# Two buffers for the first snapshot of a pair, and one address phase for both sides of SBUF

## The chip, the cores and the metric

The kernel runs on one core of one Trainium2 chip. The metric is the device time of one execution in microseconds (us), lower is better. Three executions of the kernel before took 2232.48, 2235.39 and 2237.11 us; their median is 2235.39. A fourth one was recorded by the profiler, and every row below is of that one.

The engines: PE is the matrix engine, which multiplies a moving tile (in SBUF) with weights loaded into it (also from SBUF) and sums into PSUM; PEld is its weight load. DVE, ACT and POOL are the vector, scalar and general engines; SP issues most of the DMAs.

## The reference

A decoder trunk of two layers on x of 1024 tokens by 1024 features, float32. Layer 0 mixes tokens with a chunked causal gate, layer 1 with causal differential attention over shared keys and values. Behind each mixer stands the same feed-forward block:

```python
def swiglu(h, w_gu, w_down):
    gu = h @ w_gu                       # 1024 x 1024 by 1024 x 5632
    g, u = jnp.split(gu, 2, axis=-1)
    return (jax.nn.silu(g) * u) @ w_down   # 1024 x 2816 by 2816 x 1024

for l in range(2):
    x = x + (gmlp_mixer if l < 1 else diff_attention)(rms_norm(x, ...), ...)
    x = x + swiglu(rms_norm(x, ffn_norm[l]), ffn_w_gu[l], ffn_w_down[l])
return rms_norm(x, final_norm)
```

## The kernel before

**Stages.** By the profiled execution's clock, in us: the gate branch z (34 to 92), its multiplier u (107 to 205), their output projection (205 to 310), feed-forward up of layer 0 (310 to 771), down of layer 0 (to 985), the v projection (997 to 1087), K and Q projections inside the attention (1112 to 1500), output (to 1560), up of layer 1 (1560 to 2009), down of layer 1 (to the end).

**Three products for one.** Each float32 operand is split into a high and a low part (tiles named ...h and ...l, or `w_hi` and `w_lo`): ACT casts the high part, DVE subtracts it. High times high, high times low and low times high are summed in PSUM. All these are matmuls of 512 or 256 columns (L39 is the one line through which all of PE's work goes).

**Up.** `w_gu` is cut into 11 chunk pairs j; each has a gate part (g, index 0) and an up part (u, index 1). A product by Strassen's method (Winograd's form) takes the place of eight block products. Pair 0 is done by `unit`, pairs 1 to 10 by `pair`. Names in `pair`: `B11`, `T1`, `T2`, `T3`, `B22` are blocks or sums of blocks of the activations, and at once the names of the products with them; two further products, with `B21` and `T4`, are cut once more (class `Finer`, products `mul` 1 to 7 of 256 columns, whose moving tiles are also called `fine`). A pair has 120 matmuls of 512 columns (12 for each of B11, T1, T2, T3, B22, for g and for u) and 84 of 256 columns. A product's weights are made just before it by `weight` (L304 to 310 of the kernel before): a copy into a stage (`row`, `near` or `po`, L306), a cast (L307), a subtraction (L308), into one of four `wg` buffers.

**Snapshots.** PSUM is short, so ACT copies a bank into SBUF by `snap` (L318 to 321) as soon as its product is done, and the next product is summed into the same bank:

```python
def snap(name, src):
    r = op.tile([P, 512], F32, name=name)
    A.copy(r, src)
    return r
```

The pool `op` has one buffer for each name, so c110 of a pair can be written only when the pair before is through with its c110. In a pair the names are c110 (after B11 of g), c220 (after T1 of g), c120 (after T2 of g: T2 is summed onto B11 in the bank of c110), c111 (after B11 of u), c221, c210, c121, c211. DVE later adds further banks to them (`add`, L461), and at the end of a pair POOL multiplies g by u (`store`, L340) and forms four sums (`store_sums`, L349), which SP writes to memory (`ascr`). These sums are written into the tiles c221, c121, c111, c211 (s1 to s4), and read c110, c120, c210, c220. In time this happens while the next pair has begun.

**What sets the order.** A scheduler that simulates the engines puts the instructions of all engines in an order at build time, from dependencies, buffers and modelled durations. PE's order is written by hand in the other stages; in pairs 1 to 10 the scheduler orders PE too. Every engine then runs its own list in order and waits where its next instruction is not yet free to go.

**Sides of SBUF.** Pools are laid from the left end of SBUF upwards or (function `right`, L78) from the right end downwards. In the kernel before, the left tiles that PE reads begin at multiples of 64 bytes, the right ones at 32 bytes past such multiples. Which tiles of activations stand right: in layer 0 T3, B22, B21, B11; in layer 1 T4, T3, B22 (L242, L244); `wg` is left in both. In z and u the token tiles are right and the weights left. In the v projection the weights are left, the first half of the tokens left and the second half right. In K and Q the weights are right, the tokens again half and half.

Of the kernel before, what the change touches and what calls it, by code (L numbers as in the profile page):

```python
# [9 lines left out]
F32 = mybir.dt.float32  # L10
# [6 lines left out]
P = 128  # L17
# [51 lines left out]
def trunk(ctx, tc, out, x, a_norm, w_z, w_u, gv, w_spT, b_sp, w_out, ffn_norm, w_gu, w_down,  # L69
# [5 lines left out]
    def pool(stack, name, bufs=1, **kw):  # L75
        return stack.enter_context(tc.tile_pool(name=name, bufs=bufs, reuse_waits="tile", **kw))

    def right(stack, name, bufs=1):  # L78
        return pool(stack, name, bufs, side="right")

    const = ctx.enter_context(tc.tile_pool(name="const", bufs=1))
    sm = pool(ctx, "small", 4)
    xs = pool(ctx, "xs", 8)

# [156 lines left out]
    def ffn_up(entry, layer, ascr):  # L241

        with ExitStack() as st:
# [5 lines left out]
            w1, op, sp, raw1, raw0 = (ps[n] for n in ("w1", "s", "S", "raw1", "raw0"))  # L249
# [49 lines left out]
            def weight(src, name):  # L299

                w = w1.tile([P, 2, *src.shape[1:]], F32R, name="wg")
                if name[1] == layer and name[2] == 0:
                    T.note(line, name, split(w[:, 0], w[:, 1], src))
                    return w  # L304
                near = stage().rearrange("p (k c) -> p k c", c=P)[:, :src.shape[1]]
                A.copy(near, src)  # L306
                A.copy(w[:, 0], src)  # L307
                T.note(line, name, V.tensor_tensor(w[:, 1], near, w[:, 0].bitcast(F32), op=ALU.subtract))  # L308
                return w

            def multiply(ps, w, b, start, name):
                for k in range(4):
                    with T.keep(line, name + (k,)):
                        T.matmul(ps, w[:, 0, k], hi[b][:, k], start=start and k == 0, stop=False, skip_group_check=not start)
                        T.matmul(ps, w[:, 0, k], lo[b][:, k], start=False, stop=False, skip_group_check=not start)
                        T.matmul(ps, w[:, 1, k], hi[b][:, k], start=False, stop=k == 3, skip_group_check=not start)

            def snap(name, src):  # L318
                r = op.tile([P, 512], F32, name=name)
                A.copy(r, src)  # L320
                return r

# [12 lines left out]
            def sum4(j, gu, a12, s2, s4):  # L335
                T.note(line, ("S4", layer, j, gu), G.tensor_tensor(s4, a12, s2, op=ALU.subtract))
# [15 lines left out]
            def unit(gu, res):  # L352

                def product(ps, src, b, start):
                    multiply(ps, weight(src, ("w", layer, 0, gu, b)), b, start, (layer, 0, gu, b))
                a11, a12, a22, s1, s2, s3, s4 = sums(0, gu)
                Z, Y, X = (p.tile([P, 512], F32, name="mm") for p in mmp)
                product(X, a11, "B11", True)
                c11 = snap(f"c11{gu}", X)
                yield  # L360
                product(Y, a12, "B21", True)
                T.note(line, ("c11", layer, 0, gu), V.tensor_tensor(c11, c11, Y, op=ALU.add))
                yield
                product(Z, s1, "T1", True)
                c22 = snap(f"c22{gu}", Z)
                sum4(0, gu, a12, s2, s4)
                yield
                product(X, s2, "T2", False)
                c12 = snap(f"c12{gu}", X)
                yield  # L370
                product(X, s3, "T3", False)
                V.tensor_tensor(c22, c22, X, op=ALU.add)
                yield
                product(Z, s4, "B22", False)
                V.tensor_tensor(c12, c12, Z, op=ALU.add)
                yield
                product(X, a22, "T4", False)
                res += [c11, c12, X, c22]
# [70 lines left out]
            def pair(j):  # L449

                c0, c1 = slice(0, 256), slice(256, 512)
                A_ = [sums(j, gu) for gu in range(2)]
                Z, X = ([mmp[i].tile([P, 512], F32, name="mm") for _ in range(n)] for i, n in ((0, 1), (2, 2)))
                W = mmp[0].tile([P, 2, 256], F32, name="mm")
                Z.append(mmp[0].tile([P, 512], F32, name="mm"))

                def product(ps, src, b, gu, start):
                    multiply(ps, weight(src, ("w", layer, j, gu, b)), b, start, (layer, j, gu, b))

                def add(c, ps):  # L460
                    V.tensor_tensor(c, c, ps, op=ALU.add)  # L461
                (a11g, a12g, a22g, s1g, s2g, s3g, s4g), (a11u, a12u, a22u, s1u, s2u, s3u, s4u) = A_
                product(X[0], a11g, "B11", 0, True)
                c11g = snap("c110", X[0])
                product(Z[0], s1g, "T1", 0, True)
                c22g = snap("c220", Z[0])
                sum4(j, 0, a12g, s2g, s4g)
                product(X[0], s2g, "T2", 0, False)
                c12g = snap("c120", X[0])
                product(X[1], a11u, "B11", 1, True)  # L470
                c11u = snap("c111", X[1])
                product(X[0], s3g, "T3", 0, False)
                add(c22g, X[0])
                product(Z[0], s4g, "B22", 0, False)
                add(c12g, Z[0])
                product(Z[1], s1u, "T1", 1, True)
                c22u = snap("c221", Z[1])
                sum4(j, 1, a12u, s2u, s4u)
                if j == 1:
                    finer("B21")  # L480
                    finer("T4")
                fa = Finer(j, "B21", a12g, a12u, (W[:, 0], W[:, 1]))
                add(c11g[:, c0], fa.mul(1))
                add(c11g[:, c0], fa.mul(2))
                fb = Finer(j, "T4", a22g, a22u, (X[0][:, c0], X[1][:, c0]))
                x = fb.mul(1)
                fb.mul(2)
                c21g = snap("c210", X[0])
                add(c21g[:, c0], x)
                product(X[1], s2u, "T2", 1, False)  # L490
                c12u = snap("c121", X[1])
                c21u = op.tile([P, 512], F32, name="c211")
                if j == 1:
                    names = [("d", layer, "T4", 3), ("f", layer, "B21")] + [(s, layer, 1, 0) for s in ("S1", "S2", "S3")]
                    T.order(line, names + [("S1", layer, 1, 1), ("S4", layer, 1, 0), ("f", layer, "T4")])
                for f, cg, cu in ((fa, c11g, c11u), (fb, c21g, c21u)):
                    f.weights(5)
                    z = f.mul(5)
                    if f is fa:
                        add(cu[:, c1], z)  # L500
                    else:
                        A.copy(cu[:, c1], z)
                for f, cg, cu in ((fa, c11g, c11u), (fb, c21g, c21u)):
                    f.weights(6)
                    add(cg[:, c1], f.mul(6))
                    add(cg[:, c1], f.mul(3))
                for c in (c11g, c21g, c22g, c12g):
                    A.activation(c, c, AF.Silu)
                product(X[1], s3u, "T3", 1, False)
                add(c22u, X[1])  # L510
                for f, cg, cu in ((fa, c11g, c11u), (fb, c21g, c21u)):
                    f.weights(7)
                    x = f.mul(7)
                    if f is fa:
                        both = cu.rearrange("p (i c) -> p i c", i=2)
                        V.tensor_tensor(both, both, x.unsqueeze(1).broadcast_to([P, 2, 256]), op=ALU.add)
                    else:
                        A.copy(cu[:, c0], x)
                        add(cu[:, c1], x)
                    x = f.mul(4)  # L520
                    if f is fa:
                        add(cu[:, c0], x)
                add(c21u, X[1])
                store(j, c11g, c11u, 0)
                store(j, c22g, c22u, 6)
                store(j, c21g, c21u, 5)
                product(Z[1], s4u, "B22", 1, False)
                add(c12u, Z[1])
                store(j, c12g, c12u)
                store_sums(j, c11g, c12g, c21g, c22g, (c22u, c12u, c11u, c21u))  # L530
# [312 lines left out]
    with ExitStack() as front:  # L843
# [190 lines left out]
        X = [mmp.tile([P, 512], F32, name="mm") for _ in range(4)]  # L1034
# [45 lines left out]
    with ExitStack() as mid:  # L1080
# [4 lines left out]
        with ExitStack() as att:  # L1085
# [34 lines left out]
            op = pool(att, "o", 2)  # L1120
# [367 lines left out]
```

## Time and profile before

| | |
|---|---|
| median of three runs | 2235.39 us |
| profiled execution | 2241.67 us |
| its span, first to last instruction | 2239.9 us |
| PE busy | 2138.2 us, 95% |
| DVE, ACT, POOL busy | 65%, 54%, 44% |
| mean granted TensorE clock | 0.988 of full speed |

The profiled execution is 6.3 us longer than the median. Times in the rows count from the first instruction of the span. A bracket at the end of a row of a timeline says how long the engine had nothing to do before that instruction and what ended it.

### The profile page before, as it was taken

To read this page: it belongs to the slowest core of one execution; us is meant where nothing else is said; L and a number is where in the kernel's file an instruction comes from. 1 tells how busy PE (TensorE), PEld (TensorE's weight loads), DVE (VectorE), ACT (ScalarE), POOL (GpSimd) and SP (SyncE) were. 2 spreads that over 40 slices of the span, in tenths; PEclk is the share of its full clock that TensorE was granted. 3 is DMA by queue.
4 is the path that set the end of the run, shared out by engine and by line. 5 is a ranking of instruction groups with operands and counts; after the bars stand their busy time and mean duration, and the time that the engine had idled before them with its cause. 6 is when DMAs were issued, how large, how long until landed. Compare 5 with 4: busy or idle time off the path is not lost.

```text
span 2239.9 us, 30192 instructions
## 1 busy us (share of the span) xinstructions
PE 2138.2 (95%) x10640; PEld 1773.1 (79%) x10640; DVE 1452.2 (65%) x2541; ACT 1218.3 (54%) x2436; POOL 976.3 (44%) x856
## 2 busy tenths in 40 slices
PE   9999888999999999999999999998899999999997
PEld 7888666888888778878788888887588888878887
DVE  5545987544545576785289889857855454548686
ACT  5323345666667534453277777644566666654462
POOL 5024568675666500243123332206867667550023
PEclk9999989999999999999999999999999999999999
DMA  4231011322323574235423233671222232249412
GB/s 160 66 118 61 21 55 71 109 95 82 116 95 113 200 298 144 87 118 158 108 76 86 85 105 108 208 271 71 71 88 101 95 118 95 107 159 345 144 52 88
DMA packets 111321, 265.85 MB, mean 119 GB/s; under 512 B 10401, under 2 KB 20641, under 8 KB 104257
## 3 DMA queue, kind: packets, MB, share of 16 engines
q1 hardware_dynamic: 93808, 224.98, 28.4%
q0 software_dynamic: 17360, 38.93, 6.2%
q8 instruction: 84, 1.38, 0.2%
q14 instruction: 69, 0.56, 0.1%
HBM read 179.47 MB, written 77.07 MB: 115 GB/s over the span
## 4 chain that ended last, share of the span: by engine, by line
PE 72%; DVE 13%; POOL 5%; issue 4%; ACT 3%; DMA 3%; SPq 0%; DVEq 0%; ACTq 0%; POOLq 0%
PE mm L39 47%; PE d L39 17%; PE sc L39 3%; PE po L39 2%; PE tr L42 2%; DMA graw<-in_w_gu 2%; DVE cut L645 1%; ACT wg L307 1%; DVE w_lo L163 1%; DVE wg L163 1%; DVE w_hi L163 1%; POOL c L340 1%; DVE E L1241 1%; ACT c L320 1%; PE tr L39 1%
## 5 line engine op out<-in xcount | busy, mean ns | idle before, releaser
L39 PE MATMUL d<-cut 128*128 128x512 f32 (+1 forms) x1788 | 407.1, 387 | 12.0 <-DVE cut L645 10.0
L39 PEld LDWEIGHTS d<-cut 128*128 128x128 f32 x1788 | 331.2, 189 | 84.7 <-DVE cut L645 15.0
L461 DVE TENSOR_TENSOR c<-c,mm 128x256 f32<-128x256 f32 (+1 forms) x300 | 152.0, 507 | 170.0 <-PE mm L39 119.0
L136 POOL TENSOR_TENSOR acc<-acc,sq 128x512 f32<-128x512 f32 (+1 forms) x64 | 91.4, 1430 | 374.8 <-ACT sq L132 372.9
L308 DVE TENSOR_TENSOR wg<-row,wg 128x512 fp32r<-128x512 f32 x180 | 118.0, 660 | 116.1 <-ACT wg L307 111.8
L39 PE MATMUL mm<-hT_hi,w_hi 128*128 128x512 f32 x384 | 155.9, 406 | 0.0
L39 PE MATMUL mm<-hT_lo,w_hi 128*128 128x512 f32 x384 | 151.7, 395 | 0.0
L39 PE MATMUL mm<-hT_hi,w_lo 128*128 128x512 f32 x384 | 151.4, 394 | 0.0
L39 PE MATMUL mm<-fine,wg 128*128 128x256 f32 x960 | 133.1, 284 | 18.2 <-DVE c L461 18.2
L39 PEld LDWEIGHTS mm<-fine,wg 128*128 128x128 f32 x960 | 125.9, 190 | 27.4 <-ACT c L320 19.7
L644 ACT CAST cut<-a 128x512 fp32r<-128x512 f32 x110 | 68.1, 620 | 145.7 <-PE d L39 141.2
L320 ACT COPY c<-mm 128x512 f32<-128x512 f32 x152 | 88.9, 587 | 95.6 <-PE mm L39 66.0
L645 DVE TENSOR_TENSOR cut<-a,cut 128x512 fp32r<-128x512 f32 x110 | 90.9, 827 | 72.4 <-ACT cut L644 72.0
L39 PE MATMUL mm<-T3h,wg 128*128 128x512 f32 x352 | 120.7, 405 | 3.0 <-ACT c L320 2.6
L39 PE MATMUL mm<-T1h,wg 128*128 128x512 f32 x352 | 117.8, 397 | 5.5 <-DVE wg L308 2.3
L330 POOL TENSOR_TENSOR S<-graw 128x512 f32<-128x512 f32 x44 | 59.4, 1350 | 144.5 <-DMA graw<-in_w_gu 144.5
L39 PE MATMUL mm<-B22h,wg 128*128 128x512 f32 x352 | 119.5, 401 | 2.6 <-ACT c L320 1.7
L39 PE MATMUL mm<-B11h,wg 128*128 128x512 f32 x352 | 118.8, 398 | 2.4 <-ACT wg L307 1.9
L39 PE MATMUL mm<-T2h,wg 128*128 128x512 f32 x352 | 119.5, 402 | 0.5 <-DVE wg L163 0.4
L1245 ACT ACTIVATE E<-E,nm 128x256 f32<-128x256 f32 (+7 forms) x128 | 99.6, 778 | 33.3 <-DVE nm L1241 31.9
L340 POOL TENSOR_TENSOR c<-c,c 128x512 f32<-128x512 f32 x80 | 104.6, 1309 | 29.3 <-DVE c L461 25.5
L349 POOL TENSOR_TENSOR c<-c,c 128x512 f32<-128x512 f32 x88 | 114.6, 1316 | 1.0 <-PE mm L39 0.7
(287 smaller groups left out, 5786.5 us busy)
## 6 DMA issues: line engine op xcount, KB each, us to landing
graw<-in_w_gu SPq DMA_DIRECT2D x44, 1024.0 KB, 4.9
ascr<-c SPq DMA_DIRECT2D x154, 256.0 KB, 2.0
a<-ascr SPq DMA_DIRECT2D x12, 1280.0 KB, 6.3
a<-ascr SPq DMA_DIRECT2D x18, 768.0 KB, 4.7
xscr<-x SPq DMA_DIRECT2D x48, 256.0 KB, 2.1
w<-in_w_down SPq DMA_DIRECT2D x14, 768.0 KB, 9.0
a0b<-ascr SPq DMA_DIRECT2D x12, 768.0 KB, 5.8
x<-xscr SPq DMA_DIRECT2D x16, 512.0 KB, 11.5
```

The source lines that it names most:

```text
L39: return self._keep(self.engine.matmul(*args, **kw))
L136: return (V if last else G).tensor_tensor(self.acc, self.acc, part, op=ALU.add)
L163: return V.tensor_tensor(lo, src, hi.bitcast(F32), op=ALU.subtract)
L308: T.note(line, name, V.tensor_tensor(w[:, 1], near, w[:, 0].bitcast(F32), op=ALU.subtract))
L320: A.copy(r, src)
L330: T.note(line, ("S1", layer, j, gu), G.tensor_tensor(s1, a21, a22, op=ALU.add))
L340: (G if j else V).tensor_tensor(g, g, u, op=ALU.mult)
L349: G.tensor_tensor(to, x, y, op=op_)
L461: V.tensor_tensor(c, c, ps, op=ALU.add)
L644: A.copy(o[:, 0], src)
L645: T.note(line, name + ("lo",), V.tensor_tensor(o[:, 1], src, o[:, 0].bitcast(F32), op=ALU.subtract))
L1245: A.activation(Em[:, :L], Em[:, :L], AF.Exp, scale=-1.0, bias=nm, accum_out=acc)
```

## The change

First, `snap` takes a number of buffers. c110 of the pairs gets two, and so does c11 of the g unit of pair 0 (which has the same name, c110). Second, a tile of 32 bytes per partition, named `even`, is put at the right end of SBUF ahead of everything else there, so that all right tiles stand 32 bytes lower. Now both sides begin at multiples of 64 bytes. No tile changes its side.

```diff
     const = ctx.enter_context(tc.tile_pool(name="const", bufs=1))
+    right(ctx, "even").tile([P, 8], F32, name="even")
     sm = pool(ctx, "small", 4)
...
-            def snap(name, src):
-                r = op.tile([P, 512], F32, name=name)
+            def snap(name, src, bufs=1):
+                r = op.tile([P, 512], F32, name=name, bufs=bufs)
                 A.copy(r, src)
                 return r
...
                 product(X, a11, "B11", True)
-                c11 = snap(f"c11{gu}", X)
+                c11 = snap(f"c11{gu}", X, 2 - gu)
...
                 product(X[0], a11g, "B11", 0, True)
-                c11g = snap("c110", X[0])
+                c11g = snap("c110", X[0], 2)
```

The instructions stay the same; what changes is their order, in pairs 1 to 10 of both layers and at the entries to the two down stages. (Line numbers below L82 are one higher in the changed kernel, and buffer numbers four higher.) On ACT, in a steady pair of layer 0, the stretch from the weights of T3 to the snapshot of c111. Before:

```order
L307 CAST wg_4452<-S3_4355 128x512
L306 COPY row_4471<-S4_4354 128x512
L306 COPY row_4489<-S1_4366 128x512
L307 CAST wg_4470<-S4_4354 128x512
L306 COPY row_4512<-graw_4352 128x512
L320 COPY c220_4411<-mm_4370 128x512
L307 CAST wg_4488<-S1_4366 128x512
L306 COPY row_4537<-graw_4352 128x512
L320 COPY c111_4450<-mm_4372 128x512
L307 CAST wg_4511<-graw_4352 128x512
L320 COPY c110_4392<-mm_4371 128x512
L306 COPY row_4560<-S2_4365 128x512
```

In the changed kernel:

```order
L321 COPY c110_4396<-mm_4375 128x512
L308 CAST wg_4456<-S3_4359 128x512
L307 COPY row_4475<-S4_4358 128x512
L307 COPY row_4493<-S1_4370 128x512
L308 CAST wg_4474<-S4_4358 128x512
L307 COPY row_4516<-graw_4356 128x512
L321 COPY c220_4415<-mm_4374 128x512
L308 CAST wg_4492<-S1_4370 128x512
L321 COPY c120_4435<-mm_4375 128x512
L308 CAST wg_4515<-graw_4356 128x512
L307 COPY row_4541<-graw_4356 128x512
L321 COPY c111_4454<-mm_4376 128x512
```

The snapshot of c110 now stands ahead of the weights of T3 instead of ten instructions later; c120 stands ahead of c111, c220 keeps its place. On PE, with the snapshot earlier, T2 of g follows B11 of u directly, and B22 of g comes after it. Later in the pair, at the finer products 5 and 6 (`mul`; 6 of fa and 5 of fa share one PSUM bank, and DVE reads product 5 between them), the order before is:

```order
L39 MATMUL mm_4372<-T2h_2405,wg_4559 128x512
L39 MATMUL mm_4508<-fine_2940,wg_4579 128x256 x2
L39 MATMUL mm_4371<-T4h_2411,wg_4536 128x256
L39 MATMUL mm_4371<-T4l_2412,wg_4536 128x256
L39 MATMUL mm_4371<-T4h_2411,wg_4536 128x256 x2
L39 MATMUL mm_4371<-T4l_2412,wg_4536 128x256
L39 MATMUL mm_4371<-T4h_2411,wg_4536 128x256
L39 MATMUL mm_4508<-fine_2940,wg_4579 128x256 x4
L39 MATMUL mm_4508<-fine_2943,wg_4603 128x256 x6
L39 MATMUL mm_4533<-fine_2961,wg_4591 128x256 x6
L39 MATMUL mm_4372<-T3h_2409,wg_4645 128x512
```

In the changed kernel:

```order
L39 MATMUL mm_4376<-T2h_2409,wg_4563 128x512
L39 MATMUL mm_4512<-fine_2944,wg_4583 128x256 x6
L39 MATMUL mm_4537<-fine_2965,wg_4595 128x256 x6
L39 MATMUL mm_4512<-fine_2947,wg_4607 128x256 x6
L39 MATMUL mm_4376<-T3h_2413,wg_4649 128x512
```

Here `fine` with `wg_4579` (now `wg_4583`) is product 5 of fa, with `wg_4603` (`wg_4607`) product 6 of fa, with `wg_4591` (`wg_4595`) product 5 of fb. Product 5 of fb has moved between 5 and 6 of fa, and product 2 of fb (the T4 rows) has gone ahead. On POOL the last g-times-u product (c210, L340) moves ahead of S2 and S3 of u and of the two first end sums of the pair before (L349), which stood ahead of it. SP issues the load of the next raw weights (`graw`) earlier in the pair. At the end of layer 1's up stage the casts of the first down operands (`cut`, L644) stand later on ACT, and at the end of layer 0's the weights `w3` of the down stage are loaded after all eight loads of `x`, instead of between them.

## Rows read from the trace of the kernel before

**Rows 1.** Page: PE's busy time; the chain that ended last, by engine

```profile
PE 2138.2 (95%) x10640; PEld 1773.1 (79%) x10640; DVE 1452.2 (65%) x2541; ACT 1218.3 (54%) x2436; POOL 976.3 (44%) x856
...
PE 72%; DVE 13%; POOL 5%; issue 4%; ACT 3%; DMA 3%; SPq 0%; DVEq 0%; ACTq 0%; POOLq 0%
```

**Rows 2.** Windows: length, busy us and instructions by engine, PEclk, DMA share, GB/s

```profile
439.56:755.83 316.27, 308.25 (x1632) 260.93 (x1633) 153.91 (x273) 207.63 (x393) 207.22 (x192) 1.00 0.29 106
1636.32:1952.20 315.88, 307.43 (x1633) 260.76 (x1633) 154.01 (x273) 207.68 (x393) 207.02 (x192) 1.00 0.28 101
1952.20:1996.02 43.82, 40.17 (x205) 33.78 (x205) 21.30 (x38) 27.61 (x53) 25.88 (x24) 0.96 0.45 151
```

**Rows 3.** Waits, 439.56 to 755.83: us in total, times, longest us

```profile
PEld mm L39 <- ACT c L320: 15.0, 25, 1.1
PE mm L39 <- DVE c L461: 7.3, 8, 0.9
ACT c L320 <- DMA ascr<-c: 6.0, 8, 1.8
...
ACT c L320 <- POOL c L349: 5.0, 10, 0.6
```

**Rows 4.** Timeline of PE (start, us, instruction) around product 6 of a pair

```profile
555.94 0.40 PE L39 MATMUL mm<-T4h,wg 128*128 128x256 f32 x2
...
556.42 0.64 PE L39 MATMUL mm<-fine,wg 128*128 128x256 f32 x4
557.97 1.66 PE L39 MATMUL mm<-fine,wg 128*128 128x256 f32 x12 [0.91 <-DVE c L461]
```

**Rows 5.** Timeline of DVE, same place

```profile
556.80 0.69 DVE L308 TENSOR_TENSOR wg<-row,wg 128x512 fp32r<-128x512 f32 x1 [2.18 <-ACT wg L307]
557.41 0.87 DVE L461 TENSOR_TENSOR c<-c,mm 128x256 f32<-128x256 f32 x2
```

**Rows 6.** Timeline of ACT: snapshots c220, c111, c110 of one pair

```profile
538.46 0.59 ACT L320 COPY c<-mm 128x512 f32<-128x512 f32 x1
...
541.76 0.59 ACT L320 COPY c<-mm 128x512 f32<-128x512 f32 x1 [0.55 <-DMA ascr<-c]
...
543.45 0.59 ACT L320 COPY c<-mm 128x512 f32<-128x512 f32 x1 [0.56 <-POOL c L349]
```

**Rows 7.** Timeline of PE: last product of B11 u and the one behind

```profile
536.18 0.40 PE L39 MATMUL mm<-B11h,wg 128*128 128x512 f32 x1
...
538.75 0.40 PE L39 MATMUL mm<-B11h,wg 128*128 128x512 f32 x1
539.11 0.50 PE L39 MATMUL mm<-B22h,wg 128*128 128x512 f32 x1
```

**Rows 8.** Windows in the v projection

```profile
1020.74:1043.14 22.40, 22.40 (x98) 18.02 (x96) 14.78 (x12) 8.07 (x11) 14.04 (x10) 1.00 0.63 163
1043.14:1064.95 21.81, 21.81 (x98) 18.02 (x97) 2.77 (x4) 2.35 (x4) 2.98 (x4) 1.00 0.37 96
1064.95:1087.35 22.40, 22.40 (x98) 18.02 (x97) 2.77 (x4) 2.35 (x4) 4.09 (x6) 1.00 0.39 97
```

**Rows 9.** One tile's matmuls: ns min/median/max; in u, then two tiles in the pairs

```profile
L39 PE MATMUL mm<-hT_hi,w_lo x120: 391/397/400, 109.9 to 203.7; 128*128 128x512 f32 x120
...
L39 PE MATMUL mm<-T1h,wg x128: 387/389/398, 454.5 to 742.4; 128*128 128x512 f32 x128
...
L39 PE MATMUL mm<-B11h,wg x128: 391/397/400, 451.0 to 736.6; 128*128 128x512 f32 x128
```

**Rows 10.** Timelines of ACT and PE in layer 1's last pair

```profile
1983.80 1.25 ACT L644 CAST cut<-a 128x512 fp32r<-128x512 f32 x2 [1.90 <-DMA a<-ascr]
...
1985.59 0.50 PE L39 MATMUL mm<-T3h,wg 128*128 128x512 f32 x1 [2.56 <-ACT c L320]
```

**Rows 11.** Entry to layer 0's down stage: a window, timelines of SP and PE

```profile
765.00:800.00 35.00, 34.00 (x156) 28.17 (x157) 18.32 (x30) 12.37 (x22) 8.95 (x7) 1.00 0.91 336
...
786.60 6.32 SPq L599 DMA_DIRECT2D w<-in_w_down  x3
792.97 3.67 SPq L111 DMA_DIRECT2D x<-xscr  x4
...
803.03 2.11 PE L39 MATMUL d<-cut 128*128 128x512 f32 x8 [1.87 <-ACT cut L644]
808.40 5.77 PE L39 MATMUL d<-cut 128*128 128x512 f32 x17 [3.25 <-DVE cut L645]
```

**Rows 12.** Timelines of POOL and SP: end sums, S1 of u, weight loads

```profile
537.13 2.54 POOL L349 TENSOR_TENSOR c<-c,c 128x512 f32<-128x512 f32 x2
539.62 1.30 POOL L340 TENSOR_TENSOR c<-c,c 128x512 f32<-128x512 f32 x1
...
523.87 1.31 POOL L330 TENSOR_TENSOR S<-graw 128x512 f32<-128x512 f32 x1 [7.46 <-DMA graw<-in_w_gu]
...
518.89 3.69 SPq L327 DMA_DIRECT2D graw<-in_w_gu  x2
```

## The prediction

> **What bounds the kernel now.** I read the page's busy times and the chain first [rows 1]: PE is busy 95% of the span, and 72% of the chain is PE itself. So the kernel can win only what PE loses in waits, or what its matmuls take too long. Where it waits was read next. The pairs are the largest regular piece. From product 6 of fa in one pair to that in another, eight periods of layer 0 take 316.27 us and eight of layer 1 take 315.88 [rows 2], that is 39.53 and 39.49 us each, with PE busy 308.25 / 8 = 38.53 and 38.43: one microsecond of each has no matmul at all. ACT, DVE and POOL are busy 26, 19 and 26 us of 39.5 in layer 0, so none of them is a bound by its sum; they hurt by the order in which they do things.
>
> What a pair would take with no wait comes from its matmuls. Eleven starts of B11 lie between 536.18 and 538.75 [rows 7], 233.6 ns from one to the next. 96 matmuls of one window of the v projection take 21.81 us, 227.2 ns each [rows 8]. Four matmuls of 256 columns start between 555.94 and 556.42 [rows 4], 120 ns each. In a pair of layer 0, B11, T3 and B22 (72 matmuls) have tile and weights on different sides, T1 and T2 (48) on the same; for the second kind I choose 229 ns, between this 227.2 and the 233.6 and nearer the row of the same kind. 72 x 0.2336 + 48 x 0.229 + 84 x 0.120 = 16.8 + 11.0 + 10.1 = 37.9 us. So the waits cost 39.53 - 37.9 = 1.6 us a pair, more than the idle 1.0, because a matmul whose weights come late is also recorded as longer: 0.50 us for the first of B22 against 0.40 of the one before it [rows 7].
>
> **Which waits these are.** Two [rows 3]. PE waits for DVE once a pair, 0.91 us, at product 6: it has to sum into the bank that holds product 5 until DVE has read it, and DVE does the subtraction of another weight first (0.69 us from 556.80) and reads only at 557.41 [rows 4, 5]. And the weight load waits for ACT's snapshots about three times a pair (25 times, 15.0 us, part of it beside running matmuls). The snapshots of ACT stand in a row that two things hold up [rows 6]: c111 waits for the store of the old c111 to leave (0.55 us here), and c110 for POOL to have read the old one (0.56). c110 is what T2 of g waits for, and c120 comes behind it.
>
> **The change part by part.**
>
> *Second buffer of c110.* No instruction is added. ACT no longer waits for POOL at c110, and that snapshot stands ten instructions earlier. T2 of g moves ahead of B22 of g, and product 5 of fb moves between 5 and 6 of fa; its six matmuls of 120 ns give DVE 0.72 us of cover, and the DVE read took 0.42 of the row's 0.87 for two. So the 0.91 us goes to 0 or, if DVE is late by another weight subtraction (0.69), to 0.6. What is late next is B22 of g: it needs c220, which still waits for POOL's s1 of the pair before. I placed the new order by the rows' durations, from the start of B11 of g (an estimate): T1 of g ends at 22 x 0.229 = 5.0 us, B22 of g starts 24 matmuls later, at 10.5; POOL comes to c210 at about 3.8, and with c210, S2, S3 and s1 at some 1.27 us each s1 ends at 8.9; c220 (0.59) ends at 9.55, 0.95 us early. c120 has 2 us. I take 0.4 us a pair for waits that this hand placement misses; the bounds are 0 and the 1.6 of today.
>
> *Address phase in the pairs.* In layer 0, 72 matmuls a pair change from different sides to one address phase, in layer 1, 48 (T3, B22). The v projection shows the price [rows 8]: 96 equal matmuls take 22.40 us with the tokens on the right and the weights on the left, 21.81 with both left, and 22.40 again with the tokens right, at one clock; 0.59 / 96 = 6.1 ns each. The tiles agree in kind: B11 (different sides) has a median of 397 ns, T1 (same) 389, in the same pairs [rows 9]. In a pair I take 4.6 ns (233.6 less 229): 0.33 us in layer 0, 0.22 in layer 1. The cause could be the side instead of the phase, since no row has different sides with one phase; that is the first rival. The bounds are 0 and 6.1 ns.
>
> With both, a pair takes 120 x 0.229 + 84 x 0.120 = 37.56 us, plus the 0.4: 38.0. Eight times 39.53 - 38.0 and eight times 39.49 - 38.0 give 12.2 + 11.9 = 24.1 us. The period ahead of 439.56 is another of the same kind: 1.5.
>
> *The last period of layer 1* takes 43.82 us at a clock of 0.96 [rows 2]. ACT sits 1.90 us before a cut for the down stage, waiting for its load, with the snapshot of c210 behind it; PE waits 2.56 us for that snapshot [rows 10], and the clock falls after the wait. In the new order the cuts stand behind the weights that come later. I take 38.5, so 5.3 us; the bounds are 1.5 (the wait turns up elsewhere) and 6.
>
> *Address phase elsewhere.* z and u: 2 x 384 matmuls, all with tokens right and weights left, 397 ns median in u [rows 9]: 768 x 6.1 ns = 4.7 us. v: its two windows of 22.40 us, 192 x 6.1 = 1.2 us. K, Q and the output projection: half of 1152 matmuls are affected, between others, priced at half (bounds 0 and 6.1): 576 x 3 = 1.7. Pair 0 and first parts of pair 1 in both layers: some 170 at 4.6: 0.8. Together 8.4 us, bounds 0 and 11.
>
> *Entry to the down stage of layer 0.* DMA is full there (share 0.91), and PE waits twice, 1.87 and 3.25 us, for cuts [rows 11]. The w3 loads now stand behind the second four loads of x, which SP takes 3.67 us to issue. They come later by that or more, while DVE's list is a little better placed. I take +1 us, bounds -2 and +5.
>
> The 32 bytes themselves cost nothing: the copies, casts and sums keep their shapes, and the one address phase is what the left side has already.
>
> **The sum.** -24.1 - 1.5 - 5.3 - 8.4 + 1 = -38.3 us. The profiled execution, 2241.67, would become 2203.4. It stands 6.3 us over the median of the runs; the same steps from 2235.39 give 2197.
>
> **The rivals.**
>
> *1. The phase is worth nothing.* The cost goes with the sides and not with the phase, so moving the right side by 32 bytes leaves it. For it: no row shows the phase by itself. Against: nothing else that the rows show would set the right side apart. Then 8.4 us outside the pairs stay and in them 8 x (0.33 + 0.22) = 4.4: 2197 + 13 = 2210. The Trainium skill has a rule of this kind on "SBUF — State Buffer", section "Who interferes with whom": PE reads the moving operand and the weights through two independent ports, and "PE and ACT never wait on anyone". By that rule neither phase nor side would matter; the trace doesn't agree that where the tiles stand is without effect, 22.40 against 21.81 us for the same matmuls [rows 8].
>
> *2. The snapshots' wait only moves.* c220 and c120 and c111 still have one buffer, the first waits for the same POOL sums and the last for the same store; PE waits there as long as now. For it: c111's wait on the store is larger than c110's on POOL, 6.0 against 5.0 us [rows 3]. Against: T2 of g no longer stands behind them. Pairs then gain the phase alone (4.4 us), and the last period 2: 8.4 + 4.4 + 2 - 1 = 14, so 2221.
>
> *3. Slower: POOL becomes late.* The c210 product (1.30 us) now stands ahead of S2 and S3 of u and of s1 and s3 [rows 12], and POOL waits for a raw load of 1 MB before S1 of u, 7.46 us of idle, with 3.69 us from SP's issue. If c210's factors or that load come late, S2, S3 and s1 slide, then ACT's c220 with every snapshot and weight cast behind it, and PE stands at B22 of g. It costs nothing up to 0.95 us, then its full length per pair. Without the pairs' gain (and the last period's) the rest gives -7.4 us, so the kernel is slower by over 4.5 us once each of 17 pairs takes 0.7 us more than today, that is 39.5 + 0.7 - 37.56 = 2.65 us of stall, s1 late by 3.6 us. At 5 us late a pair has 4.05 of stall, 41.6 us: 17 x 2.1 - 7.4 = +28, 2264. Against: the raw load is issued earlier in the new order, and POOL has 13 us of idle in a period.
>
> **Chances.** About what a measurement of this kernel can tell from no change is 0.2%, 4.5 us. The forecast case 0.62 (2185 to 2205), the first rival 0.12, the second 0.17, the third 0.06 (of which 0.05 is slower by over 4.5 us), and 0.03 for small mixtures around no change. Faster by over 0.2% then has 0.91, within 0.2% 0.04, slower 0.05. The low end, 2184, is all pairs at 37.56 (7 us more), the phase at its upper bound everywhere (4), and the entry at -2; the high end, 2224, takes in the second rival.
>
> **What would show it.** The period from product 6 to product 6 near 38.0 us in both layers; no DVE wait of PE at product 6; B11, T3 and B22 at T1's 389 ns; the v projection's windows all near 21.8; the u tile near 389 instead of 397; no wait for c210's snapshot in layer 1's last pair. Wrong: B22 of g waiting for c220 with POOL's L349 (now L350) behind it; v windows of 22.4 that remain.

## The result and the profile after

The changed kernel takes 2203.44 us, the median of four runs (2198.42 to 2205.48), against 2234.6 for the kernel before in its four; the ratio is 0.9857, 95% interval 0.9837 to 0.9877. That is 31 us faster where 38 were forecast, and inside the range. The profiled execution took 2203.82 us, 37.9 less than the one before and within 0.4 us of the 2203.4 forecast for it; that closeness is luck, as the end of this section shows.

The page of the changed kernel: PE's busy time (us, share, instructions) and the chain that ended last; they answer to [rows 1].

```profile
PE 2118.6 (96%) x10640; PEld 1771.6 (80%) x10640; DVE 1442.2 (65%) x2541; ACT 1217.1 (55%) x2436; POOL 980.5 (45%) x856
...
PE 78%; DVE 11%; DMA 4%; POOL 3%; issue 2%; ACT 2%; SPq 0%; DVEq 0%; ACTq 0%; POOLq 0%
```

The windows of the pairs in the changed kernel (length, busy us by engine, granted clock, DMA share, GB/s): eight periods of each layer, the last period of layer 1, and the stretch behind it; they answer to [rows 2].

```profile
430.96:734.82 303.86, 303.57 (x1633) 261.14 (x1632) 152.69 (x272) 206.34 (x393) 207.28 (x192) 1.00 0.31 109
1615.83:1919.04 303.21, 302.40 (x1633) 260.77 (x1632) 153.61 (x274) 208.74 (x396) 207.90 (x194) 1.00 0.30 105
1919.04:1956.79 37.75, 37.75 (x206) 32.62 (x204) 19.88 (x35) 26.35 (x50) 26.45 (x24) 1.00 0.53 174
1957.74:1976.67 18.93, 16.50 (x82) 14.32 (x81) 9.83 (x18) 8.83 (x17) 3.81 (x3) 0.82 0.34 119
```

A period takes 303.86 / 8 = 37.98 and 303.21 / 8 = 37.90 us, and PE is busy in all but 0.3 and 0.8 us of eight: the pairs have become a plain row of matmuls. The waits of the same eight periods of layer 0 (us in total, times, longest) show where the snapshots' waits have gone; they answer to [rows 3].

```profile
ACT c L321 <- POOL c L350: 15.5, 8, 3.1
...
ACT c L321 <- DMA ascr<-c: 2.4, 3, 1.7
...
PEld mm L39 <- ACT c L321: 0.7, 1, 0.7
PE mm L39 <- ACT c L321: 0.3, 1, 0.3
```

ACT's wait on POOL has grown, from 5.0 to 15.5 us, and PE's weight loads wait 0.7 us for ACT where they waited 15.0. It is c220 that waits. The timelines of ACT and PE in one pair show it and c110 before it, and the first matmul that needs c220 (they answer to [rows 6]):

```profile
522.64 0.59 ACT L321 COPY c<-mm 128x512 f32<-128x512 f32 x1 [0.95 <-PE mm L39]
529.06 0.59 ACT L321 COPY c<-mm 128x512 f32<-128x512 f32 x1 [1.63 <-POOL c L350]
...
530.73 0.40 PE L39 MATMUL mm<-B22h,wg 128*128 128x512 f32 x1
```

c110 waits for nothing but its product. c220 ends at 529.65 and B22 of g starts at 530.73: 1.08 us of slack. Over the eight pairs the slack goes from 1.3 us down to nothing: in the last of them c220 waits 3.11 us for POOL, and PE stands 0.29 us before B22 of g (timelines of ACT and PE there):

```profile
720.14 0.58 ACT L321 COPY c<-mm 128x512 f32<-128x512 f32 x1 [3.11 <-POOL c L350]
...
720.77 0.50 PE L39 MATMUL mm<-B22h,wg 128*128 128x512 f32 x1 [0.29 <-ACT c L321]
```

At product 6, PE goes through 18 matmuls of 256 columns without a gap (timelines of PE and DVE, which answer to [rows 4, 5]); DVE reads product 5 at 545.62, under product 5 of fb:

```profile
544.71 2.44 PE L39 MATMUL mm<-fine,wg 128*128 128x256 f32 x18
546.98 0.39 PE L39 MATMUL mm<-T3h,wg 128*128 128x512 f32 x1
...
545.62 0.42 DVE L462 TENSOR_TENSOR c<-c,mm 128x256 f32<-128x256 f32 x1 [1.59 <-PE mm L39]
```

The address phase did much less. The windows of the v projection, 96 matmuls each with the tokens right, left, right; they answer to [rows 8]:

```profile
1004.95:1027.26 22.31, 22.31 (x97) 18.08 (x96) 14.83 (x12) 8.08 (x11) 14.03 (x10) 1.00 0.63 164
1027.26:1049.06 21.80, 21.80 (x97) 18.02 (x96) 2.77 (x4) 2.35 (x4) 2.98 (x4) 1.00 0.38 97
1049.06:1071.37 22.31, 22.31 (x97) 18.09 (x96) 2.77 (x4) 2.35 (x4) 4.07 (x6) 1.00 0.39 98
```

22.40 became 22.31: 0.09 of the 0.59 us. And at the entry to layer 0's down stage (timelines of SP and PE, which answer to [rows 11]) SP issues all of x first and the w loads after it, and PE stands 9.80 us:

```profile
762.03 9.42 SPq L112 DMA_DIRECT2D x<-xscr  x8
...
773.69 14.73 SPq L600 DMA_DIRECT2D w<-in_w_down  x6
...
789.18 7.01 PE L39 MATMUL d<-cut 128*128 128x512 f32 x21 [9.80 <-ACT cut L645]
```

Not all of the 37.9 us between the two profiled executions is the change's. Two stretches with the same order in both kernels differ by themselves. From 278.30 to 310.54 us the kernel before took 32.24 us at a clock of 0.89; the changed one took 28.14 at 1.00 (windows of before, then of after):

```profile
278.30:310.54 32.24, 29.47 (x122) 23.95 (x122) 27.21 (x38) 17.21 (x31) 12.76 (x9) 0.89 0.22 82
```

```profile
278.02:306.16 28.14, 26.22 (x121) 21.48 (x120) 26.23 (x37) 16.99 (x31) 12.76 (x9) 1.00 0.25 94
```

The last 339 matmuls took 54.3 us before and 50.7 after. Over all kernels below, whose PE order is the same in both stretches, the first took 28.1 to 31.9 us and the second 50.7 to 57.9. These two account for 4.1 + 3.6 = 7.7 us, and 37.9 - 7.7 = 30.2 is close to the 31 of the medians.

### The profile page after: what moved, and what is told of

It is laid out like the page before. It is cut to its first block, busy times and chain, and to the rows that moved or that the text cites. A ratio compares the mean times of both kernels' runs of the same rounds, so it can differ in the third digit from the quotient of the medians.

```text
span 2202.1 us, 30208 instructions
## 1 busy us (share of the span) xinstructions
PE 2118.6 (96%) x10640; PEld 1771.6 (80%) x10640; DVE 1442.2 (65%) x2541; ACT 1217.1 (55%) x2436; POOL 980.5 (45%) x856
## 4 chain that ended last, share of the span: by engine, by line
PE 78%; DVE 11%; DMA 4%; POOL 3%; issue 2%; ACT 2%; SPq 0%; DVEq 0%; ACTq 0%; POOLq 0%
PE mm L39 54%; PE d L39 15%; PE sc L39 3%; PE po L39 2%; PE tr L42 2%; DVE cut L646 1%; DVE wg L164 1%; DMA w<-in_w_down 1%; DVE w_lo L164 1%; DVE w_hi L164 1%; DMA a<-ascr 1%; DVE E L1242 1%; PE tr L39 1%; DVE x L160 1%; DVE E L1254 1%
## 5 line engine op out<-in xcount | busy, mean ns | idle before, releaser
L39 PE MATMUL mm<-fine,wg 128*128 128x256 f32 x960 | 138.5, 285 | 4.4 <-DVE c L462 3.5
L39 PEld LDWEIGHTS mm<-fine,wg 128*128 128x128 f32 x960 | 130.5, 191 | 14.0 <-ACT wg L308 3.9
L308 ACT CAST wg<-S 128x512 fp32r<-128x512 f32 x160 | 99.2, 620 | 50.0 <-PE mm L39 49.3
L341 POOL TENSOR_TENSOR c<-c,c 128x512 f32<-128x512 f32 x80 | 103.5, 1304 | 31.0 <-DVE c L462 31.0
```

The lines of the kernel that those rows point to most:

```text
L39: return self._keep(self.engine.matmul(*args, **kw))
L341: (G if j else V).tensor_tensor(g, g, u, op=ALU.mult)
```

## The experiments

My theory after the result (A): the two parts are separate. The second buffer, with the order that follows from it, takes the waits out of the pairs. The tile of 32 bytes gains little, because what counts is the address over a longer stretch than 64 bytes: the left tiles begin at 320 modulo 512, the right ones at 480 before and at 448 after, 160 and 128 bytes apart. The rivals: what is left of the difference goes with the side (B); any relieved snapshot brings the gain (C). The first four ran on one chip beside the kernel before, 2232.55 us there.

**Only the tile.** The order of instructions is that of the kernel before.

```diff
     const = ctx.enter_context(tc.tile_pool(name="const", bufs=1))
+    right(ctx, "even").tile([P, 8], F32, name="even")
```

> Only the 32-byte tile; one buffer for c110. The order of instructions is that of the kernel before on every engine. The changed kernel's v projection still shows 22.31 us for 96 matmuls with the tokens right and 21.80 with them left, so 32 bytes alone took 0.9 of 6.1 ns. Theory A (what matters is the phase of the two sides over a longer stretch than 64 bytes; after the change the sides are 128 bytes apart): 2904 matmuls x 1.2 ns = 3.5 us less than before, about 2231; pairs stay at 39.3 us or more. The prediction's own price (6.1 ns) would give 13 us less, about 2222.

Measured: 2230.58 us, ratio 0.9989 (0.9973 to 1.0005). The pairs' window and PE's waits in it stay as they were, and the v windows are those of the changed kernel:

```profile
427.39:742.69 315.30, 307.43 (x1634) 261.02 (x1632) 154.05 (x272) 207.29 (x392) 206.96 (x193) 1.00 0.29 105
1011.38:1033.70 22.32, 22.32 (x98) 18.09 (x97) 12.46 (x12) 7.76 (x11) 13.19 (x10) 1.00 0.64 171
1033.70:1055.49 21.79, 21.79 (x97) 18.02 (x96) 2.77 (x4) 2.35 (x4) 2.97 (x4) 1.00 0.38 96
...
PEld mm L39 <- ACT c L321: 13.8, 24, 1.1
PE mm L39 <- DVE c L462: 7.3, 8, 0.9
```

So 32 bytes are worth 2 us, which these runs can't tell from nothing; eight pairs went from 316.27 to 315.30.

**Only the second buffer.** The diff of the change without the `even` line; the order is that of the changed kernel.

> Only the second buffer of c110; no 32-byte tile. The order is that of the changed kernel on every engine. Theory A: nearly the whole gain is here, 27 to 29 us less than before, about 2207; pairs at 38.1 us in layer 0 (37.93 plus 72 x 1.2 ns and some) without a wait of PE. Rival (the gain needs the phase): 2220 or more.

Measured: 2207.66 us, ratio 0.9881 (0.9856 to 0.9906). Its pairs are free of waits without the tile (windows of the pairs and of v):

```profile
432.12:735.60 303.48, 303.28 (x1633) 260.98 (x1632) 152.57 (x272) 206.55 (x393) 207.16 (x192) 1.00 0.30 109
1006.31:1028.71 22.40, 22.40 (x97) 18.02 (x96) 14.42 (x12) 8.07 (x11) 14.03 (x10) 1.00 0.60 163
1028.71:1050.52 21.81, 21.81 (x97) 18.02 (x96) 2.77 (x4) 2.35 (x4) 2.97 (x4) 1.00 0.38 97
```

24.9 us of the gain come from the buffer alone. A period is 303.48 / 8 = 37.94, not the 38.1 expected.

**Equal phase.** A tile of 160 bytes puts both sides at 320 modulo 512.

```diff
-    right(ctx, "even").tile([P, 8], F32, name="even")
+    right(ctx, "even").tile([P, 40], F32, name="even")
```

> The changed kernel with a tile of 160 bytes in place of 32, so that the tiles PE reads on both sides begin at one address modulo 512 bytes. Order as in the changed kernel. Theory A: all of the 2904 matmuls fall to 227 to 229 ns, 4.4 ns less each: 12.8 us less than the changed kernel, about 2191; both v windows 21.8 us; pairs 37.6 us in both layers. Rival B (what is left of the difference goes with the side, not with the address): 2203, v windows 22.3 and 21.8, pairs 37.93.

Measured: 2190.69 us, ratio 0.9804 (0.9781 to 0.9826), 12 us (by the ratios) to 13 under the changed kernel, as A had it. All three v windows are alike, and the medians of B11 and T1 in the pairs (397 and 389 ns in [rows 9]) meet at 389:

```profile
425.06:725.62 300.56, 299.94 (x1634) 260.83 (x1632) 152.65 (x272) 206.35 (x393) 207.07 (x192) 1.00 0.31 110
996.86:1018.62 21.76, 21.76 (x98) 18.02 (x96) 14.45 (x12) 8.09 (x11) 14.04 (x10) 1.00 0.64 169
1018.62:1040.38 21.76, 21.76 (x98) 18.02 (x96) 2.77 (x4) 2.35 (x4) 2.98 (x4) 1.00 0.38 97
1040.38:1062.14 21.76, 21.76 (x98) 18.02 (x96) 2.77 (x4) 2.35 (x4) 4.08 (x6) 1.00 0.40 100
...
L39 PE MATMUL mm<-B11h,wg x128: 388/389/398, 437.1 to 710.7; 128*128 128x512 f32 x128
...
L39 PE MATMUL mm<-T1h,wg x128: 389/389/390, 440.6 to 719.8; 128*128 128x512 f32 x128
```

B falls: the tiles stand on the same sides as before, and the difference is gone. The same kernel was timed once more beside the last experiment below and came out at a ratio of 0.9825, so that its lead over the changed kernel is 7 to 12 us by the ratios.

**The buffer to c111 instead.** With the tile of 32 bytes; the order is nearly that of the kernel before (38 of PE's instructions stand elsewhere).

```diff
-                c11g = snap("c110", X[0], 2)
+                c11g = snap("c110", X[0])
...
-                c11u = snap("c111", X[1])
+                c11u = snap("c111", X[1], 2)
```

(In pair 0 likewise.)

> The 32-byte tile, and the second buffer given to c111 (whose wait on its store was the larger one, 6.0 against 5.0 us in eight pairs) in place of c110. The scheduler then leaves the order of the kernel before nearly as it was. Theory A: what counts is the place that c110's snapshot gets in the order and T2 of g behind it; 2228 to 2232, pairs 39.0 to 39.5. Rival C (any snapshot relieved of its wait gives the gain, whatever the order): 2210 or less.

Measured: 2231.17 us, ratio 0.9993 (0.9978 to 1.0008), nothing beyond the tile's 2 us. Its waits over eight pairs:

```profile
PEld mm L39 <- ACT c L321: 14.2, 24, 1.1
PE mm L39 <- DVE c L462: 7.3, 8, 0.9
ACT c L321 <- POOL c L350: 5.9, 11, 0.6
```

The wait on the store, the larger one on ACT, is not in the list any more, and PE waits as long as before. C falls. That c110 matters because T2 of g, and the order of everything behind it, hang on it is read from the two orders: no run has the second buffer of c110 in the old order, or the new order with one buffer, so the 24.9 us are not divided between buffer and order.

**How far the phase reaches.** Three more distances between the sides, each timed in one execution: tiles of 416, 96 and 128 bytes give 256, 64 and 32 bytes modulo 512. The edit for 256 bytes is shown; the other two have 24 and 32 in place of 104.

```diff
-    right(ctx, "even").tile([P, 8], F32, name="even")
+    right(ctx, "even").tile([P, 104], F32, name="even")
```

> The changed kernel with a tile of 416 bytes: the two sides are 256 bytes apart modulo 512. If the price repeats every 256 bytes (theory A1), as with equal phase: v windows 21.8 and 21.8 us, pairs 37.6, about 2190. If it repeats every 512 (A2): v window with tokens right 22.3 us, pairs 37.9, about 2203.

> The changed kernel with a tile of 96 bytes: the sides are 64 bytes apart. If only equal phase is cheap and multiples of 64 bytes are otherwise alike (A3): 232.4 ns where tile and weights are on different sides, v window 22.3 us, about 2203. If the price grows with the distance (A4): about 229.5 ns, 22.05 us, 2196.

> The changed kernel with a tile of 128 bytes: the sides are 32 bytes apart, as far from multiples of 64 as in the kernel before (160 bytes apart). A3: 233.5 ns, v window 22.4 us, about 2206. A4: 228.5 ns, 21.9 us, 2193.

Measured: 2190.34, 2211.84 and 2211.13 us. The v windows (tokens right, then left) at 256, at 64 and at 32 bytes:

```profile
994.88:1016.64 21.76, 21.76 (x98) 18.02 (x96) 14.87 (x12) 8.09 (x11) 14.06 (x10) 1.00 0.64 165
1016.64:1038.40 21.76, 21.76 (x98) 18.02 (x96) 2.77 (x4) 2.36 (x4) 2.97 (x4) 1.00 0.37 97
```

```profile
1008.25:1030.65 22.40, 22.40 (x98) 18.05 (x96) 14.44 (x12) 8.08 (x11) 14.04 (x10) 1.00 0.62 165
1030.65:1052.44 21.79, 21.79 (x98) 18.02 (x97) 2.77 (x4) 2.35 (x4) 2.98 (x4) 1.00 0.38 97
```

```profile
1003.78:1026.17 22.39, 22.39 (x97) 18.03 (x96) 14.79 (x12) 8.08 (x11) 14.03 (x10) 1.00 0.62 162
1026.17:1047.94 21.77, 21.77 (x97) 18.02 (x96) 2.77 (x4) 2.35 (x4) 2.97 (x4) 1.00 0.38 97
```

At 256 bytes the price is gone as at 0, so it repeats every 256 (A1). At 32, 64 and 160 bytes it is the full one (22.39 to 22.40), at 128 a little less (22.31). A3 is right that only equal phase is cheap, and wrong that multiples of 64 are otherwise alike; A4 falls. The single times at 64 and 32 bytes are some 4 us above the median of the kernel with only the second buffer (160 bytes), whose own runs went from 2205 to 2212. The last 339 matmuls took 6.2 and 3.6 us more in these two executions than in that kernel's profiled one, so the excess is no sign of a higher price.

**w3 ahead of half of x.** On top of equal phase, in layer 0 (loads 4 to 7 of x are issued after `w3_load`; PE's order is unchanged):

```diff
-            load(W3, weight(0, 1))
+            w3_load = load(W3, weight(0, 1))
...
-                xt = new_x(xscr)
+                xt = new_x(xscr, None if layer else w3_load.ins)
```

> The kernel with equal phase (160 bytes, two buffers of c110) and one more edit: in layer 0's down stage the last four loads of x are issued behind the loads of w3, so that SP loads x four times, w3, x four times, as in the kernel before. Order on PE unchanged. In the kernel without it PE waits 9.47 us for a cut behind the w3 loads. Theory: the change pushed w3 behind all eight loads of x, and that alone made this wait; here it is 2 to 5 us and the kernel 5 to 7 us faster than 2190.7, about 2185. Rival (DMA is full there in any order): the wait stays at 8 us or more, 2190.

> The kernel with equal phase and two buffers of c110 once more, beside the next one, to compare the two on one chip: ratio 0.980 to before.

> The same with w3 ahead of the last four loads of x. The first look showed the stretch at the entry 5.1 us shorter (20.8 for 25.9 us), but the median of its runs was not lower. If the 5 us are kept to the end: ratio 0.978, 5 us under the kernel beside it. If they are given back (a later load, the clock): the same as the kernel beside it within 2 us, and the trace shows where.

Measured: 2191.93, ratio 0.9806 (0.9789 to 0.9822) the first time, where about 2185 was expected. The second time, beside one another, 2195.82, ratio 0.9825 (0.9807 to 0.9843), for equal phase alone (0.980 was expected) and 2187.99, ratio 0.9803 (0.9786 to 0.9819), with this edit. PE's wait at the entry without it (equal phase, first run) and with it (second run):

```profile
780.58 14.79 PE L39 MATMUL d<-cut 128*128 128x512 f32 x53 [9.47 <-ACT cut L645]
```

```profile
777.25 22.99 PE L39 MATMUL d<-cut 128*128 128x512 f32 x93 [4.18 <-ACT cut L648]
```

Over the same 60 matmuls the stretch takes 25.8 and 25.7 us without the edit, and 20.8 and 19.7 with it (21.0 in the kernel before): that the order of the loads makes the wait is shown. What reaches the end is not settled: nothing by the ratios of the first time, 5 us by those of the second, and the two ratios of equal phase alone differ by as much. In the first profiled execution with the edit it was given back elsewhere: against that of equal phase, 3.7 us behind the last period of layer 1 and 3.7 in the last 339 matmuls, where PE's order is the same. Up to those last 339 matmuls the profiled executions took 2130.8 and 2133.9 us without the edit and 2131.7 and 2126.9 with it.

## Why the prediction was right, point by point

**Waits in the pairs: right.** Second buffer, c110 early, T2 of g ahead of B22 of g, product 5 of fb as cover for DVE: each shows in the trace. The slack of c220, placed by hand at 0.95 us (its own terms, 8.9 and 0.59 from 10.5, give 1.0), is 1.08 in the pair shown and 0 to 1.3 over eight. The 0.4 us that I kept for missed waits was not needed: 0.3 us of idle PE in eight periods.

**The 38.0 us of a period: right for two wrong reasons.** 37.98 and 37.90 were measured, 25.1 us less over sixteen periods (forecast 24.1). But I counted 37.56 for matmuls at equal phase and 0.4 of waits; there are hardly any waits, and the 72 matmuls are still dear. With phase equal in fact, a period of layer 0 is 300.56 / 8 = 37.57.

**Address phase: the step that failed.** "6.1 ns each" was the right price of different sides (0.59 to 0.62 us for 96 matmuls in the four kernels with 32, 64 or 160 bytes), and the step from it to this change was wrong: that both sides at multiples of 64 bytes is one phase. It takes 256. The 32 bytes moved the distance from 160 to 128, worth 0.9 ns in v, so the 8.4 us outside the pairs were 1.3 by that price. The u tile, forecast near 389 ns, fell from 397 to 393. In the pairs the 32 bytes show next to nothing (303.48 us for eight periods without the tile, 303.86 with it): B11, forecast at 389, fell from 397 to 394, but T1, which stands on one side with its weights, rose from 389 to 393 (tiles of the changed kernel, ns min/median/max, in u and in the pairs; they answer to [rows 9]):

```profile
L39 PE MATMUL mm<-hT_hi,w_lo x123: 390/393/404, 108.3 to 203.6; 128*128 128x512 f32 x123
...
L39 PE MATMUL mm<-T1h,wg x128: 387/393/399, 446.6 to 729.0; 128*128 128x512 f32 x128
...
L39 PE MATMUL mm<-B11h,wg x128: 387/394/404, 443.1 to 720.1; 128*128 128x512 f32 x128
```

I had the first rival for this ("the phase is worth nothing", 2210) and argued against it with a row that shows the price only; no row of before could show what distance ends it. The rival's reason is wrong too, since phase is worth 17 us once it is equal (2207.66 to 2190.69; by the second ratio of equal phase, 0.9825 against 0.9881, some 12.5). The Trainium skill's page "SBUF — State Buffer", section "Who interferes with whom", says "PE and ACT never wait on anyone" and calls PE's read ports for the moving operand and for the weights independent. The v windows do not agree that the placing of the two is without effect: 21.76 against 22.31 to 22.40 us for the same 96 matmuls, 2.5 to 2.9%.

**The last period of layer 1: a second step that failed.** The period fell by 6.1 us (43.82 to 37.75; forecast -5.3), but the stretch behind it took 18.93 us, at a clock of 0.82, where the same matmuls took 14.75 before (first row below). PE waits there for DVE, which waits for a cut that waits for its load (the other two rows, of the changed kernel): the wait that I had as "turns up elsewhere". Some 2 us remain between the two profiled executions, and executions of one order differ by as much: period and stretch together, 286 matmuls, took 58.9 us in the kernel before, 56.2 and 57.3 in the two kernels above with its order or nearly so (only the tile, the buffer to c111), 56.9 in the changed kernel and 57.3 with only the second buffer. So no gain is shown here.

```profile
1996.33:2011.08 14.75, 13.65 (x82) 11.94 (x81) 8.86 (x17) 7.30 (x15) 4.57 (x4) 1.00 0.47 165
...
1958.47 0.62 ACT L645 CAST cut<-a 128x512 fp32r<-128x512 f32 x1 [1.55 <-DMA a<-ascr]
...
1960.29 1.21 PE L39 MATMUL mm<-fine,wg 128*128 128x256 f32 x6 [1.91 <-DVE c L462]
```

**Entry to the down stage:** forecast +1 with +5 as the bound; the stretch grew by 4.7 us (21.0 to 25.7), for the reason given, w3 behind x.

**Rival 2** ("the wait only moves") happened on ACT and hardly on PE: c220 waits 15.5 us in eight periods, inside its slack in seven of the eight pairs. **Rival 3**, whose sign was B22 of g waiting for c220 with POOL behind it, showed once in them, at 720.77, for 0.29 us; it is far from the 2.65 us a pair that would have made the kernel slower.

**The sum.** 38 became 31. Less than forecast came from the phase (7 us), the entry (4) and the last period with the stretch behind it (3). More than forecast came from the pairs (25.1 for 24.1), the period ahead of them (2.4 for 1.5) and two places that the sum left out: the first part of layer 1's up stage (1.6 us) and the end of layer 0's. For the second, matmuls 3401 to 3560 of PE's list, before and after:

```profile
745.66:778.33 32.67, 29.52 (x161) 24.92 (x160) 18.21 (x31) 17.09 (x34) 13.27 (x12) 1.00 0.66 222
```

```profile
727.39:756.51 29.12, 27.76 (x161) 24.42 (x160) 16.36 (x31) 16.50 (x34) 11.51 (x11) 1.00 0.73 238
```

Of these 3.5 us, 2.0 lie inside the eight periods counted above. Behind them, up to the first matmul of the down stage, 15.2 us became 13.7; the three kernels with the order of before or nearly so took 15.2 to 16.6 there, the others 13.5 to 16.1, so this gain is not clear of the spread. In the kernel before PE waits there for DVE, before a matmul of T4:

```profile
765.80 0.39 PE L39 MATMUL mm<-T4h,wg 128*128 128x256 f32 x1 [2.04 <-DVE c L461]
```

The 1 us or so that is left is spread over the attention and the output, in pieces that differ as much between executions of one order.

## What to carry to other kernels

Judge a wait by what hangs behind it in the order, not by its length: relieving the longer wait (c111) gave nothing, relieving c110 let the scheduler turn the pair into a row without gaps. A cost seen between two places has a period that a single pair of places can't show; before a change rests on it, try more distances. Here the tiles that PE reads at once should begin at one address modulo 256 bytes, for some 7 to 12 us more than the change brought (by the ratios of the two times that it was measured).

## What the runs showed of the hardware

- In the v projection a 512-column matmul (tiles of type fp32r) takes 226.7 ns when its moving tile and the weights lie at the same address modulo 256 bytes, and 232.4 (128 bytes apart) to 233.3 (32, 64 or 160 apart) otherwise; 256 apart is as good as 0. Whether the moving tile collides with its own weights or with those loaded for the next matmul isn't told apart here.
- A matmul's own two tiles do not settle its price. T1's matmuls in the pairs of layer 0 have tile and weights on the left, at the same address modulo 512 in every kernel; their median is 389 ns with only the second buffer and 393 in the changed kernel, where only the right side has moved by 32 bytes, and 389 again with equal phase. What they collide with isn't shown.
- With the same order, the last 339 matmuls took 50.7, 54.3 or 57 to 58 us from one execution to another. In the kernel before's (54.3) PE waits there some 3 us for DVE's `kept` and `cut`, in the changed kernel's (50.7) it does not; what makes DVE late isn't shown. So two profiled executions can differ by several us that no edit made.
